# A hybrid encoder trunk: another order of the last two attention branches' stages in the mixer

## The chip, the cores and the metric

The kernel runs on one core of a Trainium2 chip, in one launch. The metric is device time in microseconds. Before the change it is 920.55 us, the median of three runs (919.97 to 920.74). Engines are called as the profile calls them: PE (TensorE's matmuls; PEld its weight loads), DVE (VectorE), ACT (ScalarE), POOL (GpSimd) and SP (SyncE, which here only issues DMAs).

## The reference

Two layers, each on 256 positions of width 1024 in float32. The change lies in the mixer, which holds three attention branches:

```
h = RMSNorm(x);  proj = h @ w_in       # columns: latents, dq, dk, dv, sq, skv, three gates
A  o_mla : 8 heads, softmax(q k^T) v                       (latent attention)
B  o_diff: 4 heads, (softmax_1 - lam * softmax_2) v, RMS-normed per head, with ALiBi
C  o_win : 8 heads on 2 key/value heads, |t-s| <= 128, sink logit, ALiBi
x = x + (g0*(o_mla@wb0) + g1*(o_diff@wb1) + g2*(o_win@wb2)) @ w_out
```

Behind it come a gated MLP with a width-3 convolution and a per-layer input. Neither is touched.

## The kernel before, in words

**Matmuls.** Every float32 operand is split into a high and a low part of a reduced type (`split`, lines 366 to 373: ACT makes the high part, DVE the low one by a subtraction), and a product is three matmuls: high by high, high by low, low by high. Weights come in units of 512 KB by DMA (`raw`), in the order in which they are used. ACT splits off `whi` (line 91) and DVE `wlo` (line 103), each ahead of use, in pools of four buffers. A unit of a projection is 12 matmuls of 512 columns: two blocks of 128 rows of weights, two halves of the positions (128 rows each), three products. A gate `g..` has four units, a branch projection `b..` two.

**Branch stages.** `ms`, `mp`, `mo` (A), `ds`, `dp`, `do`, `dt` (B) and `ws`, `wp`, `wo` (C) are scores with softmax, turning of the probabilities on PE, output, and, in B, turning of the output. In names `L0d3s0` and `L0d3s1` are the two score banks of layer 0's differential head 3, `L0da3` its finished map (the difference of the two softmaxes), `L0da3pt` that map turned, `L0da3h` and `L0da3l` its two parts, `L0do3` its output. `L0w0s0` and `L0w0s1` are scores of the window branch's first pair of heads. `Tsq` and `Tskv` turn C's queries and keys (`L0wqb`, `L0wkb` on PE).

**Scores in pairs.** `scores2` (line 940) serves `ds` and `ws`. The contraction is only 64 deep, so two score banks take one half of PE's rows each: its loops issue a matmul for bank 0 (rows 0 to 63) and one for bank 1 (rows 64 to 127) in turn, six for each bank, 12 of 256 columns in all.

**What sets the order.** The string `ORDER` (line 52) lists the mixer's stages; the loop at the end of `layer` emits them in that order. `T...` tokens also run the scalings that were put off (`defer`) and that PE waits for (`whole`: all matmuls of a turning wait for the scaling that is last). The engines' final order is not that of the emission: the framework's scheduler lists, for each engine, whichever instruction its own cost model has ready, by priority. It is shown by a listing of the built program, engine by engine; it is fixed when the program is built, with the semaphores that an instruction waits for.

**Buffers.** Matmuls write into PSUM tiles of 512 columns, here called banks: four for projections (`pacc`), four for everything else (`psm`); a turning, a score pair or an output can only start when a bank is free. Softmax numerators lie in `tmp` tiles, the map's two halves are finished one after the other on DVE (lines 1014 to 1025): row maximum with ALiBi for both maps (1014), exponentials on ACT (1019), reciprocals (1022), factors (1023, 1024), difference (1025).

Of the kernel before, what the change touches and what calls it, by code (L numbers as in the profile page):

```python
# [50 lines left out]

ORDER = """
g00 g00 cT g00 g00 g01 ukv0 uq0 g01 g01 Tmk0 g01 Tmq0 uq1 dq ukv1 dq dq dq ms0 Tmk1 ms1 dk Tmq1 mp0 dk dk mp1
dk Tdq dv ms2 mo0 ms3 dv mp2 dv Tdk mp3 dv sq ms4 mo1 ms5 sq sq mp4 sq mp5 ms6 skv mo2 mp6 skv ms7 mp7 ds0 mo3
b00 Tsq Tskv b00 dp0 ds1 b01 b01 do0 g10 ds2 g10 dp1 do1 g10 dt0 ds3 g10 dp2 g11 dt1 do2 dp3 ws0 g11 g11 do3
g11 dt2 wp0 b10 ws1 dt3 wo0 b10 ws2 b11 b11 g20 wp1 ws3 g20 wp2 g20 wo1 g20 wo2 wp3 b20 g21 wo3 b20 g21 g21
Tmg0 g21 b21 b21
"""
# [69 lines left out]
def kernel(ctx: ExitStack, tc: tile.TileContext, a: dict, out: bass.AP):  # L128
# [29 lines left out]
    def small(n, name, bufs=None):  # L158
        return sm.tile([P, n], F32, tag=f"sm{n}", name=name)
# [364 lines left out]
    def layer(l):  # L524
# [404 lines left out]
        def scores2(q, k, jq, jk, name):  # L929

            bs = [bank(f"{name}s{e}").rearrange("p (a n) -> p a n", a=2) for e in range(2)]
            for qt in range(NT):
                qs = slice(qt * P, (qt + 1) * P)
                for n, (iq, ik) in enumerate(((0, 0), (0, 1), (1, 0))):
                    for e in range(2):
                        ro = slice(e * 64, e * 64 + 64)
                        MM(bs[e][:, qt, :], q[ro, iq, jq, qs], k[ro, ik, jk, :], start=n == 0, stop=n == 2)
            return bs

        pt_ = {}  # L940
# [64 lines left out]
        def ds(h):  # L1005
            q, k = dT["q"], dT["k"]
            at = tmp.tile([P, NT, S], F32, tag="p", name=f"{n_}da{h}")
            bs = scores2(q, k, h, h, f"{n_}d{h}")
            for qt in range(NT):
                nm = f"{n_}d{h}{qt}"  # L1010
                p2 = tmp.tile([P, 2, S], F32, tag="p", name=nm + "s")
                nmx = small(2, nm + "nm")
                for m in range(2):
                    nc.vector.tensor_tensor_reduce(out=p2[:, m, :], in0=bs[m][:, qt, :], in1=nd[:, qt, :],
                                                   scale=-SLOPES[8 + h], scalar=3.0e38, op0=ALU.add, op1=ALU.min,
                                                   accum_out=nmx[:, m:m + 1])
                sums = small(2, nm + "su")
                for m in range(2):
                    nc.scalar.activation(p2[:, m, :], p2[:, m, :], AF.Exp, bias=nmx[:, m:m + 1], scale=-1.0,
                                         accum_out=sums[:, m:m + 1])  # L1020
                r = small(2, nm + "r")
                nc.vector.reciprocal(r, sums)
                nc.vector.tensor_scalar(r[:, 1:2], r[:, 1:2], g["nlam"], None, op0=ALU.mult)
                nc.vector.tensor_scalar(p2[:, 0, :], p2[:, 0, :], r[:, 0:1], None, op0=ALU.mult)
                last = nc.vector.scalar_tensor_tensor(at[:, qt, :], p2[:, 1, :], r[:, 1:2], p2[:, 0, :], op0=ALU.mult,
                                                      op1=ALU.add)
            pt_["d", h] = at, last if h == 0 else None

        def dp(h):
            pt_["d", h] = softmax_T(pt_["d", h], f"{n_}da{h}")  # L1030
# [82 lines left out]
        for c in range(2):  # L1113
            posts[f"mq{c}"] = lambda c=c: T_mla("q", c)
            posts[f"mk{c}"] = lambda c=c: T_mla("k", c)
        stages = {"ms": ms, "mp": mp, "mo": mo, "ds": ds, "dp": dp, "do": do, "dt": dt, "ws": ws, "wp": wp, "wo": wo}
        live = {}
        for at, tok in enumerate(PLAN):
# [88 lines left out]
        for h in range(2):  # L1207
            with tc.high_priority(offset=HI):
                transpose_half(xn, h, fT[h][:, :, 0, :], fT[h][:, :, 1, :],
                               lambda k, h=h: gT[:, R_FFN + 4 * h + k:R_FFN + 4 * h + k + 1], n_ + "ffn", k_base=0)  # L1210
# [34 lines left out]
        for s in range(NF // 2):  # L1245
# [30 lines left out]
            sq = tmp.tile([P, 512], F32, tag="t512", bufs=3, name=f"{n_}c2{s}")  # L1276
# [94 lines left out]
```

## Time and profile before

| | |
|---|---|
| median of three runs | 920.55 us |
| the profiled execution | 921.1 us, of which the span is 919.3 us |
| PE busy | 906.6 us (99%) |
| DVE, ACT busy | 735.3 us (80%), 627.1 us (68%) |
| mean granted TensorE clock | 0.997 |

A busy PE is no PE at its peak: a matmul's row lasts from its start to its modelled end, and the next one starts long before. A wait shorter than that overlap shows no idle time. So waits on PE are read here from one start to the next.

### The profile page before, as it was taken

What the parts mean: (1) busy time and instruction counts of PE and PEld (TensorE: products, weight loads), DVE (VectorE), ACT (ScalarE), POOL (GpSimd) and SP (SyncE); (2) the same over time, 40 slices, a digit from 0 to 9 for tenths busy, and PEclk for the clock granted to TensorE, in tenths of its full rate; (3) what the DMA queues carried; (4) which work ended last, traced back from release to release, by engine and by line L of the source; (5) the groups of instructions that cost most, each with busy time, mean ns of one, the idle gap of its engine ahead of it and who ended that gap; (6) DMA issues with size and microseconds to landing.
All of it is one profiled execution on the core that took longest, in us unless ns stands there. A gap on an engine that the chain in (4) does not pass through costs nothing.

```text
span 919.3 us, 13722 instructions
## 1 busy us (share of the span) xinstructions
PE 906.6 (99%) x4816; PEld 766.8 (83%) x4816; DVE 735.3 (80%) x1351; ACT 627.1 (68%) x1170; POOL 81.3 (9%) x148
## 2 busy tenths in 40 slices
PE   8999999999999999999999999999999999999997
PEld 7788887888788888888888888778887888888886
DVE  5799799887688778777777987989767977777784
ACT  5778876885476566565676789688655766566572
POOL 0423110010010000000112312000000100000010
PEclk9999999999999999999999999999999999999999
DMA  7655435355646666566545645344465565656642
GB/s 221 209 181 156 142 100 163 113 168 193 193 136 212 193 192 187 187 187 200 159 146 178 203 139 163 101 151 124 138 215 170 166 205 184 200 182 193 197 149 88
DMA packets 101437, 155.90 MB, mean 170 GB/s; under 512 B 7046, under 2 KB 58104, under 8 KB 101368
## 3 DMA queue, kind: packets, MB, share of 16 engines
q1 hardware_dynamic: 101348, 155.01, 54.4%
q8 instruction: 38, 0.62, 0.3%
q14 instruction: 31, 0.25, 0.1%
q10 hardware_dynamic: 20, 0.01, 0.0%
HBM read 153.95 MB, written 1.05 MB: 169 GB/s over the span
## 4 chain that ended last, share of the span: by engine, by line
PE 86%; DVE 7%; DMA 2%; ACT 2%; issue 1%; POOL 1%; SPq 0%; ACTq 0%; DVEq 0%; POOLq 0%
PE L0g L341 7%; PE L1g L341 7%; PE L0u L341 7%; PE L1u L341 7%; PE L1dn L341 7%; PE L0dn L341 7%; DVE wlo L103 3%; DMA raw<-in_w_in_dram 2%; PE L0g20a L341 1%; PE L1g20a L341 1%; PE L1g11a L341 1%; PE L0g11a L341 1%; PE L1dva L341 1%; PE L0dva L341 1%; PE L0dka L341 1%
## 5 line engine op out<-in xcount | busy, mean ns | idle before, releaser
L103 DVE TENSOR_TENSOR wlo<-raw,whi 128x1024 fp32r<-128x1024 f32 (+3 forms) x292 | 349.1, 1205 | 89.0 <-ACT whi L91 85.9
L91 ACT ACTIVATE whi<-raw 128x1024 fp32r<-128x1024 f32 (+3 forms) x292 | 301.6, 1043 | 123.7 <-PE L0dn L341 13.2
L341 PE MATMUL L0u<-L0fT,whi 128*128 128x512 f32 x176 | 44.2, 392 | 0.0
L341 PE MATMUL L1u<-L1fT,whi 128*128 128x512 f32 x176 | 44.2, 392 | 0.0
L341 PE MATMUL L0g<-L0fT,whi 128*128 128x512 f32 x176 | 44.1, 391 | 0.0
L341 PE MATMUL L1g<-L1fT,whi 128*128 128x512 f32 x176 | 44.1, 391 | 0.0
L341 PEld LDWEIGHTS L0g<-L0fT,whi 128*128 128x128 f32 x176 | 32.2, 188 | 6.6 <-DVE L0fT L372 0.5
L341 PEld LDWEIGHTS L1g<-L1fT,whi 128*128 128x128 f32 x176 | 32.2, 188 | 6.6 <-DVE L1fT L372 0.5
L341 PEld LDWEIGHTS L1u<-L1fT,whi 128*128 128x128 f32 x176 | 31.7, 189 | 5.7
L341 PEld LDWEIGHTS L0u<-L0fT,whi 128*128 128x128 f32 x176 | 31.6, 189 | 5.7
L1272 ACT ACTIVATE L0c<-L0gs,gT 128x256 f32<-128x256 f32 x22 | 13.2, 602 | 19.2 <-DVE L0gs L1261 19.0
L1272 ACT ACTIVATE L1c<-L1gs,gT 128x256 f32<-128x256 f32 x22 | 13.3, 602 | 19.1 <-DVE L1gs L1261 19.0
L341 PEld LDWEIGHTS L0g<-L0fT,wlo 128*128 128x128 f32 x176 | 24.0, 190 | 1.7
L341 PEld LDWEIGHTS L1g<-L1fT,wlo 128*128 128x128 f32 x176 | 24.0, 190 | 1.7
L341 PEld LDWEIGHTS L0u<-L0fT,wlo 128*128 128x128 f32 x176 | 24.0, 190 | 1.7
L341 PEld LDWEIGHTS L1u<-L1fT,wlo 128*128 128x128 f32 x176 | 24.0, 190 | 1.7
L341 PE MATMUL L1u<-L1fT,wlo 128*128 128x256 f32 x176 | 24.5, 282 | 0.0
L341 PE MATMUL L0g<-L0fT,wlo 128*128 128x256 f32 x176 | 24.5, 282 | 0.0
L341 PE MATMUL L0u<-L0fT,wlo 128*128 128x256 f32 x176 | 24.5, 282 | 0.0
L341 PE MATMUL L1g<-L1fT,wlo 128*128 128x256 f32 x176 | 24.5, 282 | 0.0
L341 PE MATMUL L0dn<-whi,L0hh 128*128 128x512 f32 x88 | 24.3, 392 | 0.0
L341 PE MATMUL L1dn<-whi,L1hh 128*128 128x512 f32 x88 | 24.3, 392 | 0.0
(1730 smaller groups left out, 2479.6 us busy)
## 6 DMA issues: line engine op xcount, KB each, us to landing
raw<-in_w_in_dram SPq DMA_DIRECT2D x84, 512.0 KB
raw<-in_w_ffn_gate_dram SPq DMA_DIRECT2D x44, 512.0 KB
raw<-in_w_ffn_up_dram SPq DMA_DIRECT2D x44, 512.0 KB
raw<-in_w_ffn_down_dram SPq DMA_DIRECT2D x44, 512.0 KB
raw<-in_w_branch_dram SPq DMA_DIRECT2D x24, 512.0 KB
raw<-in_w_out_dram SPq DMA_DIRECT2D x16, 512.0 KB
raw<-in_w_ple_gate_dram SPq DMA_DIRECT2D x16, 512.0 KB
raw<-in_w_in_dram SPq DMA_DIRECT2D x8, 416.0 KB
```

Of the source, the lines that this page charges most:

```text
L91: ih = self.nc.scalar.activation(hi, self.raw[i][:, :m], AF.Copy)
L103: il = self.nc.vector.tensor_tensor(lo, self.raw.pop(i)[:, :m], hi.bitcast(F32), op=ALU.subtract)
L341: last_pe[0] = nc.tensor.matmul(*args, **kw)
L1272: nc.scalar.activation(c[:, i, :], pb["g"][:, i, :], AF.Identity, scale=tap(1), bias=gT[:, R_CB + ff:R_CB + ff + 1])
```

## The change

The string gets another order from `ds0` on, and `ds` makes all turnings of head 3's map wait for the map's second half, as it did for head 0 alone.

```diff
 ORDER = """
...
-dk Tdq dv ms2 mo0 ms3 dv mp2 dv Tdk mp3 dv sq ms4 mo1 ms5 sq sq mp4 sq mp5 ms6 skv mo2 mp6 skv ms7 mp7 ds0 mo3
-b00 Tsq Tskv b00 dp0 ds1 b01 b01 do0 g10 ds2 g10 dp1 do1 g10 dt0 ds3 g10 dp2 g11 dt1 do2 dp3 ws0 g11 g11 do3
+dk Tdq dv ms2 mo0 ms3 dv mp2 dv Tdk mp3 dv sq ms4 mo1 ms5 sq sq mp4 sq mp5 ms6 skv mo2 mp6 skv ms7 mp7 ds0 b00
+Tsq mo3 b00 dp0 Tskv ds1 b01 b01 do0 g10 ds2 g10 dp1 g10 do1 dt0 ds3 g10 g11 dp2 dt1 ws0 g11 do2 dp3 g11 do3
 g11 dt2 wp0 b10 ws1 dt3 wo0 b10 ws2 b11 b11 g20 wp1 ws3 g20 wp2 g20 wo1 g20 wo2 wp3 b20 g21 wo3 b20 g21 g21
...
-            pt_["d", h] = at, last if h == 0 else None
+            pt_["d", h] = at, last if h in (0, 3) else None
```

No instruction is added or dropped: the same matmuls, splits and transfers stand in another order, alike in both layers. SP's and POOL's lists stay as they are but for buffer numbers. Three places of the built order follow.

On PE, layer 0, before: the output of A's last two heads (`L0m3o`, which needs the two parts `L0m7h`, `L0m7l` of the last probabilities) directly behind the first differential scores (`L0d0s`), with a matmul of the branch projection `b00` between:

```order
L341 MATMUL L0m3o<-L0m6l,L0mv 128x256
L341 MATMUL L0m3o<-L0m7h,L0mv 128x256
L341 MATMUL L0b00a_1658<-whi_1521,L0o 128x512
L341 MATMUL L0m3o<-L0m7l,L0mv 128x256
L341 MATMUL L0m3o<-L0m7h,L0mv 128x256
```

and now, where 13 matmuls of 512 columns (`b00`, `b01`) and the turning of C's queries (`L0wqb`) stand ahead of it:

```order
L341 MATMUL L0b01a_1772<-whi_1645,L0o 128x512
L344 MATMUL L0wqb_1662<-ident,L0tok 128x128 x4
L344 MATMUL L0wqb_1669<-ident,L0tok 128x128 x4
L341 MATMUL L0b01a_1772<-wlo_1647,L0o 128x512
L341 MATMUL L0b01a_1772<-whi_1645,L0o 128x512
L341 MATMUL L0m3o<-L0m6h,L0mv 128x256
L341 MATMUL L0m3o<-L0m6l,L0mv 128x256
```

The output moved behind them; six matmuls of `b01` follow its eight, then the four turnings of the first map (`L0da0pt`), which stood behind 23 matmuls of `b00` and `b01` and the turning of the keys (`L0wkb`) before, then the rest of `b00`, which needs that output's parts (`L0o`).

On DVE, layer 0, before: the end of the first differential map (`L0da_1600`), whose second half is the row of line 1025:

```order
L372 SCALAR_TENSOR_TENSOR L0wqT<-L0wqb_1685,gT_397,L0wqT 128x512
L1022 RECIPROCAL L0d01r<-L0d01su 128x2
L809 TENSOR_TENSOR L0tok<-L0tok,L0wk0ri 128x256
L1023 TENSOR_SCALAR L0d01r<-L0d01r,gsc_400 128x1
L1024 TENSOR_SCALAR L0d01s<-L0d01s,L0d01r 128x256
L809 TENSOR_TENSOR L0tok<-L0tok,L0wk1ri 128x256
L1025 SCALAR_TENSOR_TENSOR L0da_1600<-L0d01s,L0d01r 128x256
```

and now:

```order
L1024 TENSOR_SCALAR L0d01s<-L0d01s,L0d01r 128x256
L926 TENSOR_TENSOR L0m3ot<-L0m3o,L0m3oy 64x256
L1025 SCALAR_TENSOR_TENSOR L0da_1600<-L0d01s,L0d01r 128x256
L926 TENSOR_TENSOR L0m3ot<-L0m3o,L0m3oy 64x256
L103 TENSOR_TENSOR wlo_1795<-raw_1692,whi_1793 128x1024
L369 TENSOR_TENSOR L0o<-L0m3ot,L0o 128x256
L369 TENSOR_TENSOR L0da0l<-L0da0pt,L0da0h 128x512
```

The additions that finish A's last output (line 926) came from the map's first half to its second, the key scalings (line 809) went behind it, and a weight split (line 103) stands ahead of the low part of A's output. What DVE does before that, from `L0m7l` over the query scalings (line 717) to the map's first half, kept its order, without the two additions.

On PE, layer 0, before: the scores of head 3, the two banks in turn (two and two at first, then one and one to twelve):

```order
L341 MATMUL L0g10a1_1833<-whi41_1893,L0hTh_159 128x512
L341 MATMUL L0d3s0_1964<-L0dkT_1221,L0dqT_1088 128x256 x2
L341 MATMUL L0d3s1_1965<-L0dkT_1221,L0dqT_1088 128x256 x2
L341 MATMUL L0d3s0_1964<-L0dkT_1221,L0dqT_1088 128x256
L341 MATMUL L0d3s1_1965<-L0dkT_1221,L0dqT_1088 128x256
```

and now:

```order
L341 MATMUL L0g10a1_1833<-wlo41_1895,L0hTh_159 128x512
L341 MATMUL L0d3s0_1964<-L0dkT_1221,L0dqT_1088 128x256 x6
L341 MATMUL L0g10a1_1833<-whi41_1893,L0hTl_160 128x512
L341 MATMUL L0d3s1_1965<-L0dkT_1221,L0dqT_1088 128x256 x6
L341 MATMUL L0g10a1_1833<-whi41_1893,L0hTh_159 128x512
```

Bank 0's six stand together, then a matmul of the gate `g10` on all 128 rows, then bank 1's six. The window branch's first scores (`L0w0s0`, `L0w0s1`) stand likewise now, six, one matmul of `g11`, six; before they were four, four and then in turn. All other score blocks alternate in both programs.

## Rows read from the trace of the kernel before

**Rows 1.** The page, part 1: busy time, share of the span, instructions.

```profile
PE 906.6 (99%) x4816; PEld 766.8 (83%) x4816; DVE 735.3 (80%) x1351; ACT 627.1 (68%) x1170; POOL 81.3 (9%) x148
```

**Rows 2.** The page, part 4: the chain that ended last, by engine.

```profile
PE 86%; DVE 7%; DMA 2%; ACT 2%; issue 1%; POOL 1%; SPq 0%; ACTq 0%; DVEq 0%; POOLq 0%
```

**Rows 3.** Windows, both layers' changed stretch: PE, PEld, DVE, ACT, POOL busy, clock, DMA.

```profile
123.40:172.10 48.70, 48.06 (x277) 37.92 (x273) 43.09 (x123) 36.08 (x95) 2.99 (x4) 1.00 0.40 121
574.80:623.50 48.70, 48.05 (x275) 38.10 (x271) 43.04 (x123) 36.12 (x95) 3.00 (x4) 1.00 0.39 121
```

**Rows 4.** Timeline of PE, three waits: start, length, instruction, [idle before].

```profile
123.46 0.39 PE L341 MATMUL L0m3o<-L0m6h,L0mv 128*128 128x256 f32 x1
...
124.16 0.39 PE L341 MATMUL L0b00a<-whi,L0o 128*128 128x512 f32 x1
124.78 0.39 PE L341 MATMUL L0m3o<-L0m7l,L0mv 128*128 128x256 f32 x1 [0.23 <-DVE L0m7l L369]
...
147.16 0.39 PE L341 MATMUL L0g10a<-whi,L0hTl 128*128 128x512 f32 x1
147.38 0.39 PE L341 MATMUL L0g10a<-whi,L0hTh 128*128 128x512 f32 x1
148.04 0.39 PE L341 MATMUL L0do<-L0dv,L0da1l 128*128 128x256 f32 x1 [0.27 <-DVE L0da1l L369]
...
152.19 0.48 PE L341 MATMUL L0g11a<-whi,L0hTh 128*128 128x512 f32 x1
152.81 0.55 PE L344 MATMUL L0da2pt<-ident,L0da 128*128 128x128 f32 x3
```

**Rows 5.** Timeline of PE, score blocks and what follows them.

```profile
117.84 0.88 PE L341 MATMUL L0m7s<-L0mkT,L0mqT 96*128 96x256 f32 x6
118.56 0.40 PE L341 MATMUL L0b00a<-whi,L0o 128*128 128x512 f32 x1
...
150.35 0.40 PE L341 MATMUL L0g10a<-whi,L0hTh 128*128 128x512 f32 x1
150.68 0.98 PE L341 MATMUL L0d3s<-L0dkT,L0dqT 64*128 64x256 f32 x12
151.59 0.50 PE L341 MATMUL L0g10a<-wlo,L0hTh 128*128 128x512 f32 x1
...
158.04 1.19 PE L341 MATMUL L0w0s<-L0wkT,L0wqT 64*128 64x256 f32 x12
159.16 0.50 PE L341 MATMUL L0g11a<-wlo,L0hTh 128*128 128x512 f32 x1
```

**Rows 6.** Timeline of PE, turning of the window queries.

```profile
126.88 0.63 PE L344 MATMUL L0wqb<-ident,L0tok 128*128 128x128 f32 x4
127.26 0.48 PE L341 MATMUL L0b01a<-whi,L0o 128*128 128x512 f32 x1
```

**Rows 7.** Timeline of DVE, from the query scalings to the first differential map.

```profile
126.05 0.69 DVE L717 TENSOR_TENSOR L0tok<-L0tok,L0w1tot 128x512 f32<-128x512 f32 x1
...
127.68 0.42 DVE L926 TENSOR_TENSOR L0m3ot<-L0m3o,L0m3oy 64x256 f32<-64x256 f32 x1
128.13 0.48 DVE L1025 SCALAR_TENSOR_TENSOR L0da<-L0d00s,L0d00r 128x256 f32<-128x256 f32 x1
128.53 0.42 DVE L1014 CUSTOM_DVE_ANT_0 L0d01s<-L0d0s,nd 128x256 f32<-128x256 f32 x1
...
129.22 0.42 DVE L369 TENSOR_TENSOR L0o<-L0m3ot,L0o 128x256 fp32r<-128x256 f32 x1
129.56 1.40 DVE L372 SCALAR_TENSOR_TENSOR L0wqT<-L0wqb,gT,L0wqT 128x512 fp32r<-128x512 f32 x2
130.88 0.15 DVE L1022 RECIPROCAL L0d01r<-L0d01su 128x2 f32<-128x2 f32 x1
...
131.99 0.48 DVE L1025 SCALAR_TENSOR_TENSOR L0da<-L0d01s,L0d01r 128x256 f32<-128x256 f32 x1
```

**Rows 8.** Timeline of ACT, the high part of branch A's last output.

```profile
128.13 0.42 ACT L368 ACTIVATE L0o<-L0m3ot 128x256 fp32r<-128x256 f32 x1
```

## The prediction

> **What bounds the kernel now.** I read the page's busy times and its chain first. PE is busy 99% of the span [rows 1], and 86% of the chain that ended last is PE, 7% DVE [rows 2]: the end moves with what PE has to do and with what it waits for, and another engine counts only where PE stands waiting for it. Then the windows over the stretch in which the order changes: 48.70 us in either layer, PE busy 48.06 and 48.05, DVE 43.09 and 43.04, the clock at 1.00 [rows 3]. The two layers are the same to a hundredth, so I work out layer 0 and count it twice; and DVE is busy 88% of that stretch, so that it can easily become what PE waits for. Last the timeline of PE. A row of 512 columns lasts 0.39 us but the next starts 0.22 to 0.23 behind it (147.16, 147.38), so a wait is the start-to-start time less 0.23, not the idle time in brackets [rows 4].
>
> The sum is made against the profiled execution, 921.1 us (span 919.3, 1.8 around it); the median of the runs shown is 920.55, 0.55 lower, and the time predicted is put on that.
>
> **What the change removes.** Three waits of PE in each layer [rows 4]. `L0m3o` waits for the low part of the last probabilities: 124.16 to 124.78, 0.62 - 0.23 = 0.39 us. `L0do` of head 1: 147.38 to 148.04, 0.43. The turnings of head 2: 152.19 to 152.81, 0.39. Now some 3 us of matmuls and turnings stand ahead of `L0m3o`; head 1's output stands behind a whole unit of `g10`, and its low part on DVE no longer behind the row maxima of head 2; head 2's turnings stand behind 12 matmuls of `g11`. Gone: 1.2 us a layer, 1.0 if a tenth or so stays.
>
> **What it adds: scores that no longer run in pairs.** This is work of PE itself, whatever the other engines do. The six matmuls of `L0m7s`, 256 columns on one row group, take 0.72 us to the next start, 0.12 each. The 12 of `L0d3s`, which alternate between two halves of the rows, take 0.91 to the next start (150.68 to 151.59) and not 1.44: the two halves run side by side. And the step into them costs: the matmul ahead of them is followed after 0.33 and not 0.23 [rows 5]. In the new order six of one half, a matmul on all 128 rows, and six of the other follow each other. Each half runs six steps in the 0.91 as it is, so a half alone takes the same 0.91: two of them, and one more step in of 0.10, against one: +1.0 for `L0d3s`. `L0w0s` takes 1.12 now (158.04 to 159.16), so there it is 2 x 0.91 + 0.10 - 1.12 = +0.8. Bounds: at the least a half takes what lies between first and last start plus nothing, 0.98 - 0.28 = 0.70 (0.28 being a lone matmul of that size at its end, as `L0m7s` has it, 0.88 - 5 x 0.12), which gives +0.5 and +0.3; at the most the way out costs another 0.1 each, +1.1 and +0.9. I take +1.8 a layer (0.8 to 2.0), by the row of the very block.
>
> The Trainium skill, "TensorEngine Tiling (Array Packing)", Overview, gives up to a factor of two for a contraction of at most 64, and under Key Properties lets a change of mode drain TensorE, without a price. By the factor alone a block out of pairs would cost about 0.7 more, 1.4 a layer, an estimate; the trace has a price of 0.1 for the step in besides, and it decides.
>
> **What it adds: waits.** Four places, each followed by hand with the durations of before.
>
> First the queries' turnings (`L0wqb`). They wait for the second scaling of line 717, which on DVE has nothing new ahead of it: it ends at 126.05 + 0.69 = 126.74 [rows 7], and PE now comes to them 0.1 + 13 x 0.23 behind 123.46 [rows 4], at 126.55. Before, PE came to them at about that time, 126.88 [rows 6]. New wait 0.25; the rest of PE's queue stands behind it.
>
> Second the turnings of the first map (`L0da0pt`). PE: from 126.80 eight turnings at 0.1 (0.38 for four with the step back [rows 6]), eight matmuls of 512 columns (1.84), eight of 256 (0.96), a step or two: about 130.45. DVE: the first half's line 1025 stood 2.08 behind the scaling with two additions of line 926 of about 0.4 among it (127.68 to 128.13 is one), so now at 127.35; 0.40 to the maxima of the second half, 0.69 for these (128.53 to 129.22), 1.32 for the queries' low parts (129.56 to 130.88), 1.11 from the reciprocal to line 1025 with one instruction of 0.3 between as now (130.88 to 131.99), 0.48 for itself: 131.35 [rows 7]. ACT's side is hidden in that: the queries' high parts and the exponentials end ahead of DVE's turn. New wait 0.9, where before the keys' turnings and 23 matmuls of `b00` and `b01` covered it; part of that cover now stands behind the waiting turnings. Bounds 0 and 1.2.
>
> Third `b00`, right behind those turnings: it needs the high part of A's last output, which ACT makes in 0.42 [rows 8] behind the second addition of line 926, itself 0.42 [rows 7] and now behind the map: 131.3 + 0.42 + 0.42 = 132.2, PE is there at 131.8. New wait 0.4, from 0 to 0.6. Its low part comes behind a weight split, and five matmuls cover that.
>
> Fourth, the weight splits move ahead in DVE's list: three more of them stand before the second half of head 1's map than did. By the same steps its turnings wait 0.1 and the first window scores, for the bank of head 2's turnings, 0.3 at most. I take 0.2 together, 0 to 0.5. Weights themselves are not late: the splits moved earlier, and transfers follow from freed buffers, in the same lists of SP.
>
> **Sum.** A layer: -1.2 + 1.8 + 0.25 + 0.9 + 0.4 + 0.2 = +2.35; two: +4.7. 921.1 + 4.7 = 925.8 for a profiled execution, 920.55 + 4.7 = 925.25 on the median: 925.2. With every term at its low end -1.2 + 0.8 = -0.4 a layer (919.7), at the high end -1.0 + 2.0 + 0.25 + 1.2 + 0.6 + 0.5 = +3.55 (927.7).
>
> **Rivals.**
>
> *The pairs hold, so only waits change sides (919.0).* The halves may not be bound to their place in the list: in `L0w0s` they already stand four, four and then in turn, and the block took 1.12, just 0.21 more than a paired one [rows 5]. If bank 1's six run beside bank 0's, the 1.8 is gone, and if PE is later than I have it at the first map's turnings, the new waits come to 0.4: -0.8 a layer, 918.95. It decides where the second six start within 0.2 us of the first. Against it: the matmul between them uses all 128 rows. The Trainium skill, "TensorE: Matmul & The Clock Gate", Part 3, has matmuls start and end in program order; no run here shows it for a full matmul between two halves. Chance 0.06.
>
> *Gains and losses cancel (920.8).* Blocks out of pairs at the low bound (+0.8), new waits of 0.5, three old waits gone (-1.2): +0.1 a layer, 920.75. For it: each wait depends on two engines' times to a few tenths, and a PE that is later waits less. Against it: the queries' scaling is one instruction with the same list ahead of it. Chance 0.15.
>
> *DVE becomes the bound of the stretch (928.2).* It is busy 43 of 48.7 us [rows 3]; with PE waiting at the first map, everything of DVE behind it shifts, and the weight splits now stand ahead of head 1's second half. If the maps of heads 1 to 3 then come late by 0.5 us each, 1.5 more a layer: 920.55 + 4.7 + 3.0 = 928.25. It decides where line 1025 of head 1 ends later than the unit of `g10` ahead of its turnings; by my steps it is a tenth. Chance 0.17.
>
> **How the numbers follow.** The forecast has 0.62, with 922.6 to 927.7 as its own range: half of the new waits gone, or every term high. What a measurement of this kernel can tell from no change is about 0.2%, 1.8 us. Slower are the forecast and the DVE case, 0.62 + 0.17, of which 0.02 fall within 0.2%; no change 0.15 + 0.02; faster 0.06: chances 0.06, 0.17 and 0.77. The range of 8 in 10 has to reach into the cancelling case and the DVE case: 920.4 to 928.0.
>
> **What would show it.** In the new profile `L0d3s` and `L0w0s` stand as two groups of six with a `g10` or `g11` matmul between and about 0.9 us from each first start to the next matmul; if the second six start within 0.2 us of the first, that step is wrong. `L0m3o` and head 1's `L0do` start without a wait. `L0wqb` waits for line 717 with 0.2 to 0.3, `L0da0pt` for line 1025 with about 0.9, the next `b00` for ACT with 0.4; if `L0da0pt` starts 0.23 behind the matmul ahead of it, the second wait is wrong. The stretch of the windows above, from 123.4 to the start of `L0w1s`, should take 51 us instead of 48.7. The prediction as a whole is wrong if PE's stretch gets no longer, which it would without the first step and the second.

## The result, and the profile after

The changed kernel takes 925.94 us (median of four runs, 925.57 to 926.01) against 920.26 of the kernel before beside it (919.77 to 920.74): 1.0066 of its time, 95% interval 1.0054 to 1.0078. The forecast was 925.2; as an increase it is 5.7 us beside that kernel, for 4.7 forecast on the earlier 920.55. The profiled execution's span is 924.2 us, 4.9 more than before; its start-up, ahead of anything the change touches, happened to be 0.9 shorter (the first `L0d0s` starts at 121.64, before at 122.56).

The page of the changed kernel, busy times and the chain by engine, against [rows 1, 2]:

```profile
PE 910.2 (98%) x4816; PEld 768.9 (83%) x4816; DVE 736.9 (80%) x1351; ACT 627.9 (68%) x1170; POOL 79.9 (9%) x148
...
PE 87%; DVE 6%; ACT 3%; DMA 2%; issue 1%; POOL 1%; SPq 0%; ACTq 0%; DVEq 0%
```

Neither tells where the time goes: the same instructions, and PE busy 3.6 us longer with them. The stretch does. The windows that answer to [rows 3], from 0.84 us behind the first `d0s` to the first `w1s` in either layer, columns as there:

```profile
122.48:174.29 51.81, 50.18 (x277) 39.37 (x273) 43.59 (x122) 36.15 (x95) 2.76 (x4) 1.00 0.39 113
576.79:628.55 51.76, 50.19 (x275) 39.36 (x271) 43.55 (x122) 36.16 (x95) 2.79 (x4) 1.00 0.37 113
```

51.81 and 51.76 us for 48.70: +3.1 a layer, with DVE about as busy as it was (43.6 us for 43.1) and the clock at 1.00. Up to the first turning of the merged branches (`L0mgT`, `L1mgT`) 0.2 of it is given back: from the first `d0s` to there it is 95.73 and 95.70 us, before 92.85 and 92.81. I use this longer stretch below.

PE's timeline in the changed kernel, layer 0, at the places of the forecast: start, length, instruction, [idle before]. They answer to [rows 4, 6]:

```profile
125.17 0.61 PE L341 MATMUL L0b01a<-whi,L0o 128*128 128x512 f32 x2
125.75 1.09 PE L344 MATMUL L0wqb<-ident,L0tok 128*128 128x128 f32 x8
...
126.92 0.40 PE L341 MATMUL L0b01a<-whi,L0o 128*128 128x512 f32 x1
127.20 0.38 PE L341 MATMUL L0m3o<-L0m6h,L0mv 128*128 128x256 f32 x1
...
129.42 0.39 PE L341 MATMUL L0b01a<-whi,L0o 128*128 128x512 f32 x1
130.21 0.66 PE L344 MATMUL L0da0pt<-ident,L0da 128*128 128x128 f32 x4 [0.40 <-DVE L0da L1025]
131.10 0.50 PE L341 MATMUL L0b00a<-whi,L0o 128*128 128x512 f32 x1 [0.24 <-ACT L0o L368]
...
144.38 0.40 PE L341 MATMUL L0g10a<-whi,L0hTl 128*128 128x512 f32 x1
144.95 0.55 PE L344 MATMUL L0da1pt<-ident,L0da 128*128 128x128 f32 x3 [0.17 <-DVE L0da L1025]
...
146.49 0.40 PE L341 MATMUL L0g10a<-whi,L0hTl 128*128 128x512 f32 x1
146.73 0.28 PE L341 MATMUL L0do<-L0dv,L0da1h 128*128 128x256 f32 x1
...
157.59 0.39 PE L341 MATMUL L0g11a<-whi,L0hTl 128*128 128x512 f32 x1
158.20 0.38 PE L341 MATMUL L0w0s<-L0wkT,L0wqT 64*128 64x256 f32 x1 [0.22 <-DVE L0da2l L369]
...
171.39 0.39 PE L341 MATMUL L0b10a<-whi,L0od 128*128 128x512 f32 x1
172.37 0.41 PE L344 MATMUL L0dot<-ident,L0od 128*128 128x128 f32 x2 [0.59 <-DVE L0do3m L377]
```

From start to start, less 0.23: the first map's turnings wait 0.56 us, head 1's turnings 0.34, the first window scores 0.38 (0.10 of it their step in), and the turning of head 2's output 0.75. The matmul of `b00` behind the first map's turnings starts 0.51 behind the last of them (130.21 + 0.66 - 0.27, the length of one turning, is 130.60); behind the turnings of [rows 6] the next matmul starts 0.02 to 0.03 after the last, so `b00` waits 0.48. The three waits of [rows 4] are gone: `L0m3o` starts 0.28 and head 1's `L0do` 0.24 behind the matmul ahead, and head 2's turnings start on time too.

And the scores that answer to [rows 5]:

```profile
149.69 0.39 PE L341 MATMUL L0g10a<-wlo,L0hTh 128*128 128x512 f32 x1
150.01 0.97 PE L341 MATMUL L0d3s<-L0dkT,L0dqT 64*128 64x256 f32 x6
150.92 0.50 PE L341 MATMUL L0g10a<-whi,L0hTl 128*128 128x512 f32 x1
151.35 0.97 PE L341 MATMUL L0d3s<-L0dkT,L0dqT 64*128 64x256 f32 x6
152.25 0.50 PE L341 MATMUL L0g10a<-whi,L0hTh 128*128 128x512 f32 x1
```

Each half takes 0.90 to 0.91, as a whole paired block did, and the matmul between them 0.43 instead of 0.23: a step out and a step in. From 150.01 to 152.25 that is 2.24 - 0.23 = 2.01 for 0.91: +1.10. `L0w0s` is the same, 2.01 for 1.12: +0.89.

### The profile page after: what moved, and what is told of

It reads as the page before. It is cut to its first block, busy times and chain, and to the rows that moved or that the text cites. A ratio compares the mean times of both kernels' runs of the same rounds, so it can differ in the third digit from the quotient of the medians.

```text
span 924.2 us, 13720 instructions
## 1 busy us (share of the span) xinstructions
PE 910.2 (98%) x4816; PEld 768.9 (83%) x4816; DVE 736.9 (80%) x1351; ACT 627.9 (68%) x1170; POOL 79.9 (9%) x148
## 4 chain that ended last, share of the span: by engine, by line
PE 87%; DVE 6%; ACT 3%; DMA 2%; issue 1%; POOL 1%; SPq 0%; ACTq 0%; DVEq 0%
PE L1g L341 7%; PE L0g L341 7%; PE L0u L341 7%; PE L1u L341 7%; PE L1dn L341 7%; PE L0dn L341 7%; DVE wlo L103 2%; DMA raw<-in_w_in_dram 2%; PE L1g20a L341 1%; PE L0g20a L341 1%; PE L1dva L341 1%; PE L0dva L341 1%; PE L0dka L341 1%; PE L1dka L341 1%; PE L0pg0a L341 1%
```

## The experiments

Two theories. P: the pairs and the waits add up, each at its own place. D (W in the first expectations): DVE and ACT's chain of maps sets the pace, and what PE gains at one place it waits for at the next. The last columns of the table matter for reading it: the scheduler lists DVE's and ACT's instructions anew for every edit, and how many of DVE's about 1350 rows have moved by that, against the kernel that the edit starts from, is read by comparing the listings of the two built programs. Each ratio is taken against runs of the kernel before that were made beside that kernel (their medians lie between 919.56 and 920.26), and so are the differences in us in the text.

| kernel | us | ratio to before (95%) | d0s to mgT, layers 0, 1 | start from; DVE rows moved |
|---|---|---|---|---|
| before | 920.26 | | 92.85, 92.81 | |
| changed | 925.94 | 1.0066 (1.0054 to 1.0078) | 95.73, 95.70 | before; 74 |
| e2 blocks split | 923.51 | 1.0037 (1.0025 to 1.0050) | 94.43, 94.38 | before; 15 |
| e3 halves adjacent | 920.45 | 1.0005 (0.9996 to 1.0014) | 93.02, 92.95 | before; 0 |
| e4 first part | 927.11 | 1.0075 (1.0063 to 1.0088) | 96.02, 96.31 | before; 77 |
| e5 second part | 922.26 | 1.0024 (1.0015 to 1.0033) | 93.81, 93.77 | before; 40 |
| e8 waits filled | 919.29 | 0.9994 (0.9985 to 1.0004) | 92.32, 92.35 | before; 22 |
| e10 head 1's scores late | 925.80 | 1.0058 (1.0046 to 1.0071) | 95.74, 95.77 | before; 67 |
| e11 filled, scores early | 918.88 | 0.9991 (0.9982 to 1.0000) | 92.36, 92.33 | before; 22 |
| e1 head 3 paired | 925.67 | 1.0067 (1.0053 to 1.0081) | 95.72, 95.73 | changed; 41 |
| e6 all paired | 925.22 | 1.0056 (1.0043 to 1.0068) | 95.50, 95.41 | changed; 56 |
| e7 head 2's turning late | 927.57 | 1.0084 (1.0071 to 1.0096) | 96.50, 96.59 | changed; 29 |
| e9 head 1's scores early | 923.92 | 1.0046 (1.0032 to 1.0059) | 95.04, 95.05 | changed; 71 |
| e12 halves together | 922.54 | 1.0030 (1.0018 to 1.0042) | 93.92, 94.04 | changed; 0 |

In all of them PE has the same 521 matmuls in layer 0's stretch, and their usual distances add up to about 86.5 us (285 matmuls of 512 columns at 0.227, 72 of 256 at 0.12, 68 turnings at 0.109, and eight score blocks of 12 in pairs at 0.72); the rest is waits and steps.

**The blocks split in the kernel before (e2).**

```diff
+            steps = [(qt, n, e) for qt in range(NT) for n in range(3) for e in range(2)]
+            if name[2:] in ("d3", "w0"):
+                steps.sort(key=lambda s: s[2])
...
+                if True and name[2:] in ("d3", "w0") and (qt, n, e) == (0, 0, 1):
+                    second.append([last_pe[0], 4 if name[2] == "d" else 2])
...
+                if second:
+                    second[0][1] -= 1
+                    if second[0][1] == 0:
+                        order(second.pop()[0], last_pe[0])
```

Bank 1's first matmul waits for the fourth (head 3) or second (window) step of the unit of weights that follows; so two and three full matmuls stand between the halves.

> The kernel before with its order of stages untouched, in which only the scores of differential head 3 and of the first window pair are split: six of bank 0, two (head 3) or three (window) full matmuls, six of bank 1. Theory P: +1.10 for d3s and +0.89 for w0s a layer as in the changed kernel; behind the later d3s the turnings of head 2 no longer wait (0.39 before), so +1.6 a layer, 3.2 us in all: about 923.5 (924.3 if that wait stays). Theory W: the blocks cost nothing by themselves: 920.3, within half a microsecond.

923.51, +3.6, as forecast. PE's timeline of it:

```profile
150.16 0.98 PE L341 MATMUL L0d3s<-L0dkT,L0dqT 64*128 64x256 f32 x6
151.06 0.50 PE L341 MATMUL L0g10a<-wlo,L0hTh 128*128 128x512 f32 x1
151.40 0.40 PE L341 MATMUL L0g10a<-whi,L0hTl 128*128 128x512 f32 x1
151.73 0.97 PE L341 MATMUL L0d3s<-L0dkT,L0dqT 64*128 64x256 f32 x6
152.63 0.33 PE L344 MATMUL L0da2pt<-ident,L0da 128*128 128x128 f32 x1
```

Two halves of 0.90 each, and head 2's turnings behind them no longer wait: the price less the wait that it covers.

**The halves adjacent in the kernel before (e3).** The same edit without that wait.

> The kernel before with its order of stages untouched, in which the scores of differential head 3 and of the first window pair stand six of bank 0 and then six of bank 1 with no full matmul between. It tells whether the order in the list breaks the pairs or the full matmul between the halves. Theory Q (the two row groups run side by side whatever their order in the list, as long as no matmul on all 128 rows stands between; for it, in the trace of before w0s stands 0000 1111 0101 and bank 1's first matmul starts 0.01 us ahead of bank 0's second): the second six start about 0.2 us behind the first, 920.3 to 921.1. Theory L (matmuls start in the order of the list): the second six start behind the first six, 12 steps of 0.12 instead of 6: +0.72 for d3s less the 0.39 of the wait behind it, +0.5 for w0s, 0.8 to 1.2 a layer, 922.0 to 922.7.

```profile
150.14 1.32 PE L341 MATMUL L0d3s<-L0dkT,L0dqT 64*128 64x256 f32 x12
151.39 0.50 PE L341 MATMUL L0g10a<-wlo,L0hTh 128*128 128x512 f32 x1
```

The block takes 1.25 us, between the 0.91 of pairs and the 1.63 (0.91 + 6 x 0.12) of two sixes in a row; the second six start 0.35 behind the first and run beside them from there. `L0w0s` takes 1.25 too, 0.13 more than before. 920.45: no difference that can be told, in part because the longer `L0d3s` covers the wait of 0.39 behind it, which is gone. So six and six costs a little, 0.34 and 0.13, and the full matmul between them the rest: 2.01 for 1.25.

**The two parts of the order alone (e4, e5).**

```diff
-b00 Tsq Tskv b00 dp0 ds1 b01 b01 do0 g10 ds2 g10 dp1 do1 g10 dt0 ds3 g10 dp2 g11 dt1 do2 dp3 ws0 g11 g11 do3
+Tsq mo3 b00 dp0 Tskv ds1 b01 b01 do0 g10 ds2 g10 dp1 do1 g10 dt0 ds3 g10 dp2 g11 dt1 do2 dp3 ws0 g11 g11 do3
```

(The line ahead of it ends in `ds0 b00` instead of `ds0 mo3`.)

> The first part of the new order alone (A's last output behind the queries' turning, the keys' turning behind the first map); from head 1's turnings on the order of before, without the wait of head 3's turnings for the whole map. In the built order d3s stands six and six with no full matmul between, w0s three and three and then in turn. Theory P (waits and pairs add up, each at its own place): the wait of A's output goes (-0.39 a layer), the waits of the queries', the first map's turnings and of b00 come as in the changed kernel (+0.13, +0.56, +0.41), the blocks cost nothing: +0.7 a layer, 921.3 (920.8 to 922.0). If only blocks out of pairs made the changed kernel slower, it is 919.5 or less. Theory D (the chain over DVE and ACT sets the pace of the stretch, and what PE saves it waits for further on): the late first map shifts the maps of the heads behind it, and more waits come, 922.5 or more.

```diff
-b00 Tsq Tskv b00 dp0 ds1 b01 b01 do0 g10 ds2 g10 dp1 do1 g10 dt0 ds3 g10 dp2 g11 dt1 do2 dp3 ws0 g11 g11 do3
+b00 Tsq Tskv b00 dp0 ds1 b01 b01 do0 g10 ds2 g10 dp1 g10 do1 dt0 ds3 g10 g11 dp2 dt1 ws0 g11 do2 dp3 g11 do3
...
-            pt_["d", h] = at, last if h == 0 else None
+            pt_["d", h] = at, last if h in (0, 3) else None
```

> The second part of the new order alone (head 1's output behind a unit of g10, the scores of the window branch ahead of head 2's output, and the wait of head 3's turnings for the whole map); from ds0 to ds1 the order of before. In the built order both score blocks keep their pairs (two and two, then in turn). Theory P: the waits of head 1's output (0.43) and of head 2's turnings (0.39) go and nothing comes for them but, at most, the wait of head 2's turned output seen in the changed kernel (0.75): between -0.1 and -0.8 a layer, 918.7 to 920.1, most likely 919.2. Theory S (this part of the order is what costs, pairs or not): 922 or more.

The parts cost 7.35 and 2.35 us, and 5.7 together: they don't add. The second keeps its pairs in the list, and yet I was wrong on it, and S's "922 or more" was right; PE's timeline shows why, in two waits above all:

```profile
167.13 0.39 PE L341 MATMUL L0b10a<-wlo,L0od 128*128 128x512 f32 x1
168.32 0.41 PE L344 MATMUL L0dot<-ident,L0od 128*128 128x128 f32 x2 [0.81 <-DVE L0od L1051]
...
175.15 0.39 PE L341 MATMUL L0b10a<-whi,L0od 128*128 128x512 f32 x1
175.79 0.50 PE L341 MATMUL L0b10a<-whi,L0od 128*128 128x512 f32 x1 [0.25 <-DVE L0od L372]
```

The turning of head 2's output waits 0.96 us, the unit of `b10` that needs it 0.41. Head 1's output, whose wait was to go, still waits 0.46, and the window scores 0.34 (0.10 of it their step in). In the first part alone no block is split by a full matmul, and P's +0.7 a layer came out as +3.2 and +3.5. Besides the waits forecast (0.56, and 0.49 at `b00`) head 1's turnings wait 0.34, head 3's 0.38, and the outputs of heads 2 and 3 0.2 each. The largest single item is a score block, `L0w1s`, listed six and six here: bank 1 waits for DVE's line 372, which reads out what its bank held before.

```profile
172.20 0.96 PE L341 MATMUL L0w1s<-L0wkT,L0wqT 64*128 64x256 f32 x6
173.44 0.97 PE L341 MATMUL L0w1s<-L0wkT,L0wqT 64*128 64x256 f32 x6 [0.28 <-DVE L0od L372]
```

So its halves run one after the other, and it takes 2.15 us (to 174.35) instead of 0.91. With `L0d3s` at 1.36 for 0.91 and `L0w0s` at 0.91 for 1.12 that is 1.5 of the 3.2 in layer 0: pairs are lost here as well, not to a full matmul but to a bank that comes free late. D's number, "922.5 or more", was right here.

**Head 3's scores in pairs, in the changed kernel (e1).**

```diff
+                        prev = last_pe[0]
                         MM(bs[e][:, qt, :], q[ro, iq, jq, qs], k[ro, ik, jk, :], start=n == 0, stop=n == 2)
+                        if name[2:] in PAIRED:
+                            order(last_pe[0], low_dt[PAIRED[name[2:]]] if (qt, n, e) == (0, 0, 0) else prev)
...
+        PAIRED, low_dt = {"d3": 0}, {}
...
-            split(dst[:, 0, h, :], dst[:, 1, h, :], bt[:, :S], g["do"])
+            low_dt[h] = split(dst[:, 0, h, :], dst[:, 1, h, :], bt[:, :S], g["do"])[1]
```

> The changed kernel, in which alone the scores of differential head 3 stand in pairs again: their first matmul waits for the low part of head 0's turned output (which frees the second bank), and the twelve are chained bank 0, bank 1 in turn; no full matmul stands between them. The window scores stay six, one, six. Theory P (time is lost because blocks stand out of pairs): in the changed kernel's trace d3s takes 2.01 us beside the one full matmul, 0.91 before, so 1.10 a layer come back: 2.2 us less than the changed kernel, about 923.7. Theory W (the loss is the new waits, and a block out of pairs only fills time in which PE would have waited anyhow): the waits behind it grow by what the block gives back, no gain: 925.9. If it is 1 us or less below the changed kernel, P is wrong as an account of the d3s half.

925.67: nothing gained. The block is whole again, and PE waits further on:

```profile
150.17 0.97 PE L341 MATMUL L0d3s<-L0dkT,L0dqT 64*128 64x256 f32 x12
151.07 0.50 PE L341 MATMUL L0g11a<-whi,L0hTh 128*128 128x512 f32 x1
...
154.64 0.40 PE L341 MATMUL L0g11a<-wlo,L0hTh 128*128 128x512 f32 x1
155.67 0.44 PE L344 MATMUL L0dot<-ident,L0od 128*128 128x128 f32 x2 [0.63 <-DVE L0od L1056]
...
202.86 0.39 PE L341 MATMUL L0b20a<-wlo,L0ow 128*128 128x512 f32 x1
203.54 0.50 PE L341 MATMUL L0b20a<-whi,L0ow 128*128 128x512 f32 x1 [0.29 <-DVE L0ow L369]
```

0.80 at the turning of head 1's output and 0.45 at `b20`. For a while this made D my theory. But 41 of DVE's rows had moved: a weight split of 1.22 us now stood ahead of head 1's normalisation.

**All pairs, and later turnings (e6, e7).** e6 has the edit of e1 with `"w0": 1` beside `"d3": 0`, and these lines; e7 is the changed kernel with the second line's edit alone.

```diff
-Tsq mo3 b00 dp0 Tskv ds1 b01 b01 do0 g10 ds2 g10 dp1 g10 do1 dt0 ds3 g10 g11 dp2 dt1 ws0 g11 do2 dp3 g11 do3
-g11 dt2 wp0 b10 ws1 dt3 wo0 b10 ws2 b11 b11 g20 wp1 ws3 g20 wp2 g20 wo1 g20 wo2 wp3 b20 g21 wo3 b20 g21 g21
+Tsq mo3 b00 dp0 Tskv ds1 b01 b01 do0 g10 ds2 g10 dp1 g10 do1 dt0 ds3 g10 g11 dp2 g11 dt1 ws0 do2 dp3 g11 do3
+g11 wp0 b10 dt2 ws1 dt3 wo0 b10 ws2 b11 b11 g20 wp1 ws3 g20 wp2 g20 wo1 g20 wo2 wp3 b20 g21 wo3 b20 g21 g21
```

> The changed kernel with the scores of head 3 and of the first window pair in pairs (first matmul behind the low part of the turned output that frees the second bank, then bank 0 and bank 1 in turn), head 1's turned output one unit of g11 later, head 2's turned output behind the turnings of the window branch's first heads and a unit of b10. Theory P: pairs (1.10 and 0.89) and the wait of head 2's turned output (0.75) come back, 2.7 a layer: 925.9 - 5.4 = 920.5. Theory D: as in the kernel with head 3's scores alone in pairs (925.67), PE comes earlier and waits for DVE at the next place: 924 or more.

> The changed kernel, in which only head 2's turned output stands later, behind the turnings of the window branch's first heads and a unit of b10. Theory P: its wait of 0.75 a layer goes, 925.9 - 1.5 = 924.4. Theory D: the wait comes back at the turnings or the scores behind, 925.5 or more.

925.22 and 927.57; P's 920.5 and 924.4 failed both times, and D's ranges held. In e6 the split blocks are gone, and the first window scores wait 0.40, head 3's output 0.45, head 2's turning 0.62 and `b20` 0.67; `L0w1s`, six and six now, takes 1.40 for 0.91. In e7 the wait of head 2's turning is gone, and `b20` waits 0.38 where it had none, and the block `L0w1s` takes 0.46 more (1.37), because its bank 1 comes free late. Both moved rows on DVE again (56 and 29).

**When head 1's scores start (e9, e10).** In the changed kernel they start 14.0 us behind the first `d0s` (before 10.9), and head 3's map is done after 41.2 (38.1).

```diff
-Tsq mo3 b00 dp0 Tskv ds1 b01 b01 do0 g10 ds2 g10 dp1 g10 do1 dt0 ds3 g10 g11 dp2 dt1 ws0 g11 do2 dp3 g11 do3
+Tsq mo3 b00 dp0 ds1 Tskv b01 b01 do0 g10 ds2 g10 dp1 g10 do1 dt0 ds3 g10 g11 dp2 dt1 ws0 g11 do2 dp3 g11 do3
...
+                        if name[2:] == "d1" and (qt, n) == (0, 0):
+                            order(last_pe[0], last_gemm[0])
```

> The changed kernel with head 1's scores ahead of the keys' turning, right behind the last matmul of b00, instead of behind it, b01 and five matmuls of g10. In the built order every block of scores is whole (in turn, or the two banks' six directly behind each other). Theory D (what counts is when head 1's scores start, 14.0 us behind the first differential scores in the changed kernel and 10.9 before; through the chain over DVE and ACT the maps of heads 1 to 3 come late by 1.3, 1.8 and 3.1 us, and PE waits for them or for what hangs on them wherever it is not slowed otherwise): they start about 2.5 us earlier, head 1's map is done by 22.3 us or earlier (23.3 in the changed kernel), head 3's by 39.5 (41.2), and most of the loss goes: 920.0 to 922.0. Theory P (waits and pairs add up, each at its own place): the two blocks out of pairs come back, 2.0 a layer, 921.9, with the maps where they are in the changed kernel. Theory O (the order on DVE of the first part, not the scores' place, makes the maps late): 924 or more.

```diff
+                if (name[2:], k // per, c) in behind_mm:
+                    for late in behind_mm.pop((name[2:], k // per, c)):
+                        order(late, last_pe[0])
...
+                        if name[2:] == "d1" and (qt, n) == (0, 0):
+                            behind_mm.setdefault(("g10", 0, 1), []).append(last_pe[0])
```

> The kernel before with its order of stages, in which only head 1's scores are put off behind 11 more matmuls (five of b01, six of g10; 2.5 us), by making their first two wait for the sixth matmul of g10. No block of scores has a full matmul between its halves. Theory D: head 1's map is done 1 us or more later (21.9 us behind the first differential scores before), the maps behind it too, and PE waits for them: 922.5 to 925. Theory P: no block is out of pairs and no wait of the changed kernel's first part is made: at most a few tenths a layer, 919.5 to 921.0.

In e9 the maps come earlier as D had it (22.2 and 39.0 us) but the time is 923.92, above what D and P gave and just under O's "924 or more". The score blocks are 1.2 us a layer shorter than in the changed kernel, the stretch only 0.7: the waits at the window scores (0.73), at head 2's turning (0.90) and at `b10` (0.47), which e5 has too, stay. In e10 the scores come 2.6 us later and nothing else was asked for: 925.80, as much as the whole change and above D's range too, with no block split by a full matmul. The row of DVE that ends head 3's map, in the kernel before, the changed one and e10 (their first `d0s` start at 122.56, 121.64 and 120.92):

```profile
160.15 0.48 DVE L1025 SCALAR_TENSOR_TENSOR L0da<-L0d31s,L0d31r 128x256 f32<-128x256 f32 x1
```

```profile
162.30 0.48 DVE L1025 SCALAR_TENSOR_TENSOR L0da<-L0d31s,L0d31r 128x256 f32<-128x256 f32 x1
```

```profile
162.06 0.48 DVE L1030 SCALAR_TENSOR_TENSOR L0da<-L0d31s,L0d31r 128x256 f32<-128x256 f32 x1
```

38.1, 41.1 and 41.6 us. So late scores of head 1, with the list that the scheduler makes of them on DVE, are enough to lose 5.8 us, 2.9 a layer. But not as D had it: head 1's own map, which was to be 1 us or more later, is done after 22.2 for 21.9, and the delay begins behind it. And 2.1 of the 2.9 lies in the score blocks: `L0d2s` takes 1.32, `L0d3s` 1.53 and `L0w1s` 2.15 for 0.91 to 0.92 each (`L0w0s` 0.92 for 1.12), because their second banks come free late, as in e4. In e10 too, most of the time is lost where pairs do not run as pairs.

**The three old waits filled (e8), and head 1's scores early with it (e11).**

```diff
+                    if name[2:] == "m3" and (e, kt) == (1, 0):
+                        behind_mm["b00", 1, 2] = last_pe[0]
...
+                    if (h, qt, kt) == (1, 0, 0):
+                        behind_mm["g10", 3, 1] = last_pe[0]
...
+                if name[2:] == "da2" and (kt, qt) == (0, 1):
+                    behind_mm["g11", 0, 0] = last_pe[0]
```

> The kernel before with its stages' order, in which the three waits of PE that the change removed are filled with matmuls that stood right behind them: A's last output has two more matmuls of b00 ahead of its waiting part, head 1's output the turning of head 0's output and two more of g10, head 2's turnings two more of g11. All score blocks keep their pairs. Theory P: 1.2 a layer are gained, 2.4 in all: 917.9 (917.4 to 918.8). Theory D: PE only comes earlier to the next thing that it needs of DVE and waits there: 919.3 to 920.5.

```diff
-b00 Tsq Tskv b00 dp0 ds1 b01 b01 do0 g10 ds2 g10 dp1 do1 g10 dt0 ds3 g10 dp2 g11 dt1 do2 dp3 ws0 g11 g11 do3
+b00 Tsq b00 dp0 ds1 Tskv b01 b01 do0 g10 ds2 g10 dp1 do1 g10 dt0 ds3 g10 dp2 g11 dt1 do2 dp3 ws0 g11 g11 do3
```

> The kernel with the three filled waits (919.29), in which the keys' turning stands behind head 1's scores instead of ahead of them. In the built order head 1's scores then start some 0.8 us earlier behind the first differential scores (11.3 in that kernel, 10.9 before, about 10.4 here), and all score blocks are whole. Theory D (the start of head 1's scores sets when the maps of heads 1 to 3 are done): head 3's map is done by 37.2 us (37.6 in that kernel, 38.1 before), the wait of head 2's output (0.38) shrinks, and 0.3 to 0.8 a layer are gained: 917.7 to 918.7. Theory P: nothing that PE does is less: 919.0 to 919.6.

In e8 1.2 us of waits a layer are taken away, but the stretch is only 0.5 shorter, and 919.29 is D's range, not P's; the queries' turning now waits 0.27 and head 2's output 0.38:

```profile
153.60 0.40 PE L341 MATMUL L0g11a<-whi,L0hTh 128*128 128x512 f32 x1
154.22 0.39 PE L341 MATMUL L0do<-L0dv,L0da2h 128*128 128x256 f32 x1 [0.22 <-DVE L0da2l L369]
```

In e11 head 1's scores start 1.1 us earlier and head 3's map is done at the same 37.64 us: earlier scores don't help, D's second half fell, and 918.88 lies between the two ranges. e11 is the fastest kernel of all, 0.9991 (0.9982 to 1.0000), within what a measurement can tell from no change.

**The halves together, and nothing else (e12).** The full matmul between the halves goes ahead of the block (for the window scores two more of `g11` with it), which leaves `L0d3s` listed five and five and then in turn, and `L0w0s` in turn; the lists of DVE, ACT, POOL and SP are those of the changed kernel, word for word.

```diff
+                if (name[2:], k // per, c) in behind_mm:
+                    order(behind_mm.pop((name[2:], k // per, c)), last_pe[0])
...
+                        if name[2:] in BEHIND and (qt, n, e) == (0, 0, 0):
+                            behind_mm[BEHIND[name[2:]]] = last_pe[0]
...
+        BEHIND = {"d3": ("g10", 3, 2), "w0": ("g11", 1, 2)}
```

> The changed kernel with one thing undone: the full matmul of g10 or g11 that stands between the two banks' halves of head 3's and of the first window pair's scores stands ahead of the block (two more of g11 with it), so that the halves stand together (five and five and then in turn; in turn). The rest of PE's list and the lists of all other engines are the same word for word, which they were not in the kernel with head 3's scores alone in pairs. Theory P (a block out of pairs costs its 1.10 and 0.89 a layer in the changed kernel too): 0.7 to 1.1 for d3s (five and five overlap later than pairs), 0.7 to 0.9 for w0s, so 1.4 to 2.0 a layer: 922.0 to 923.1. Theory D (behind these blocks PE comes to things that the chain over DVE and ACT has not done, and waits): the waits of w0s (0.38) and of head 2's turned output (0.75) grow by what the blocks give back: 925.0 to 925.9.

922.54, ratio 1.0030 where the changed kernel has 1.0066: 0.36% or 3.3 us come back, P's range, far from D's.

```profile
150.32 1.29 PE L341 MATMUL L0d3s<-L0dkT,L0dqT 64*128 64x256 f32 x12
151.54 0.50 PE L341 MATMUL L0g10a<-whi,L0hTh 128*128 128x512 f32 x1
...
157.91 1.33 PE L341 MATMUL L0w0s<-L0wkT,L0wqT 64*128 64x256 f32 x12
159.17 0.50 PE L341 MATMUL L0g11a<-whi,L0hTh 128*128 128x512 f32 x1
...
169.82 0.39 PE L341 MATMUL L0b10a<-whi,L0od 128*128 128x512 f32 x1
170.74 0.41 PE L344 MATMUL L0dot<-ident,L0od 128*128 128x128 f32 x2 [0.53 <-DVE L0do3m L377]
```

The blocks take 1.22 and 1.26 for 2.01 each: 1.54 a layer, and the stretch is 1.81 and 1.66 shorter. The wait of head 2's turning did not grow (0.69 for 0.75). The 0.28 ahead of the window scores is gone, and their wait now lies inside the block, which is why it takes 1.26 and not 0.91: bank 1's first matmul starts at 158.26, 0.36 behind bank 0's and just behind the end of the DVE row that reads out its bank (157.73 + 0.48 = 158.21).

```profile
157.73 0.48 DVE L372 SCALAR_TENSOR_TENSOR L0od<-L0dot,gsc,L0od 128x256 fp32r<-128x256 f32 x1
```

So e1 and e6 had not shown that PE's gain is lost to the chain in the changed kernel; they showed what happens together with another list on DVE. D holds where that list moves, as a description. Part of what it describes, in e4, e6, e7 and e10, is a score block whose second bank DVE reads out late; which of the moved rows makes that and the other waits stays open.

## Why the prediction was right, point by point

**The scores out of pairs: right.** Forecast +1.8 a layer, between 0.8 and 2.0. The blocks measure +1.10 and +0.89, together the upper bound: the matmul between the halves pays a step out of 0.1 besides the step in, which I had put at the bound only. e2 and e12 show the price without and with the rest of the change: 3.6 and 3.3 us, over half of the 5.7. (The row of `L0m7s`, from which I took 0.12 a step, is 96 rows deep and no half; but the steps inside a half are 0.12 in the changed kernel too.) The rival in which the pairs hold is out (the second six start 1.34 us behind the first); e3 shows that without the full matmul it would have come close (0.35 behind, where it asked for 0.2), so its counter-argument, the 128 rows of that matmul, was the point. The rule of the Trainium skill, "TensorE: Matmul & The Clock Gate", Part 3, that matmuls start in program order agrees with the changed kernel, where bank 1's first matmul starts 0.43 us behind the full one listed ahead of it, and not with e3, where the second bank's first matmul starts 0.35 us behind the first and the two sixes run side by side; there the measurement decides.

**The removed waits: right.** All three of [rows 4] are gone, 1.2 a layer. The place of `w1pt` gave another 0.16 that I had not looked for.

**The new waits ahead of head 1: right in place, smaller in size.** The queries' turning 0.13 for 0.25, the first map's turnings 0.56 for 0.9, `b00` 0.48 for 0.4. Together 1.2 for 1.55: the first map was done about 0.3 earlier than by my steps.

**The small ones: too low.** Head 1's turnings 0.34 for 0.1, the window scores' bank 0.28 for at most 0.3: 0.6 for 0.2.

**The step that failed: the end of the new waits.** I followed the maps to the window scores and stopped; the turning of head 2's output was not in the sum at all and waits 0.75 a layer. DVE's timeline of the changed kernel:

```profile
169.14 0.16 DVE L992 TENSOR_TENSOR L0w1de<-L0w1su,L0w1es 128x2 f32<-128x2 f32 x1 [0.74 <-ACT L0w1p L989]
169.33 0.17 DVE L909 RECIPROCAL L0w1rc<-L0w1de 128x2 f32<-128x2 f32 x1
169.41 0.41 DVE L1045 TENSOR_TENSOR L0od<-L0od,L0do 128x256 f32<-128x256 f32 x1
170.83 0.17 DVE L377 TENSOR_SCALAR L0do2m<-L0doss 128x2 f32<-128x2 f32 x1 [1.00 <-ACT L0doj L1049]
171.80 0.43 DVE L1051 TENSOR_TENSOR L0od<-L0od,L0do2r 128x256 f32<-128x256 f32 x1 [0.80 <-POOL L0do2r L379]
```

With the window scores ahead of head 2's output, the addition that begins that output's normalisation stands behind the second window head's sums, which wait for ACT; from there it goes to ACT, DVE, POOL and back, 2.8 us in a row, and PE's next work is used up by then. e5 has the same wait, 0.96, without a split block: it belongs to the second part of the order. e7 takes this wait away, but moves DVE's list with it; no run takes it away alone.

**The sum.** -1.2 - 0.16 + 2.0 + 1.2 + 0.6 + 0.75, and 0.3 given back at `b20` further on, is +2.9, as the stretch has it (+2.88 a layer), for +2.35 forecast; a single wait is read to a tenth or so. The 0.75 that I had not seen, 0.4 on the small ones and 0.2 on the pairs stand against 0.4 too much ahead of head 1 and 0.46 given back that I had not counted. That the total lies only 0.7 us under the measurement is owed to errors of both signs, and to the base: as an increase it is 1.0 short (4.7 for 5.7), and the kernel before happened to be 0.3 faster beside the changed one than in the runs that the forecast stands on.

**The rival in which DVE becomes the bound: half right.** Its condition holds: line 1025 of head 1 ends late enough for PE to wait 0.34 and not a tenth, and the maps of heads 1 to 3 are done 1.3, 1.8 and 3.1 us later behind the first `d0s`. But PE is later by then itself: it waits there for 0.6 (head 1's turnings, the window scores), 1.4 with head 2's turned output, and the price of 1.5 on top of all the forecast's waits is not reached.

## What to carry to other kernels

Two half-height score banks ran side by side here only where no full-height matmul was listed between them, and only from when both banks were free (2.01 and 2.15 us for 0.91); look for both in the built order and the trace, since an emission that alternates can be listed as six, one, six. When the order of stages moves, follow each stage's result to its last reader on PE, past the stage that was moved: the wait that was missed lay 14 us behind the window scores that had moved. And an experiment that reorders one engine is only clean when the lists of the others stand still; of the attempts to undo the pairs the one with no row of another engine moved gave 3.3 us back, and the two others less than 1.

## What was unexpected of the hardware

Twelve score matmuls on the two halves of the rows take 0.91 us listed in turn, 1.25 listed six and six with nothing between (both blocks of e3), and 2.01 listed six and six with one full matmul between, beside that matmul itself. So matmuls further down PE's list start on the idle half of the rows ahead of earlier ones: in e3 bank 1's first starts 0.35 us behind bank 0's first, ahead of bank 0's fourth (only the first matmul of a bank waits for a semaphore, which tells them apart). In none of the 14 traces does one start ahead of a full matmul that is listed before it.
